# First stage with staging slots and a written order of its loads, the scan one projection later, and the roots of the first scales partly in PSUM

## The chip, the cores and the metric

The kernel runs on one core of a Trainium2 chip. The metric is the device time of one execution in microseconds (us). Three runs of the kernel before took 1379.6, 1372.67 and 1366.87 us, median 1372.67. The profiled execution is another one; it took 1369.38 us, and its span in the trace is 1367.0 us.

## The reference

One layer of a hybrid encoder on 2048 tokens of 1024 features, all in fp32. What bears on this case:

```python
hn   = rms_norm(h, norm_pre[i])            # h = x, 2048 x 1024
proj = hn @ w_in[i]                        # 1024 x 3072
u_s, z_s, q, k, v, z_n = jnp.split(proj, splits, axis=-1)    # 512 columns each
y_s  = s5_bidirectional(u_s, ...)          # 32 groups of 16 channels, a linear scan over the tokens each way
y_s  = gelu(y_s); y_s = y_s * sigmoid(y_s @ w_glu + b_glu) * silu(z_s)
y_n  = neighborhood_attention_2d(q, k, v, rpb) * silu(z_n)
h    = h + rms_norm(concat(y_s, y_n) @ w_out, norm_post)
h    = h + sigmoid(h @ w_gate) * rms_norm(p @ w_ple, ple_norm)
```

`rms_norm` divides each token's row by the root of its mean square; that root is a scale per token, which the kernel multiplies into the result of the projection.

## The kernel before, in words

**Matmuls in two parts.** Every fp32 matmul is made of three on rounded operands: x is split into a high part `xh` and a rest `xl`, and w into `wh` and `wl`. One result tile of 128 columns x 512 tokens takes 8 slices x 3 = 24 matmuls (`dense_steps`, L205). There are four blocks of 512 tokens, so one projection of 128 columns is 96 such matmuls.

**First stage** (`start`, L230). The first three projections (the u columns 0 to 383) run together, block by block: for each block b, 72 matmuls. `load_x` (L128) brings the transposed x of a block in 8 tiles (`xr`, L137) and splits each one: ACT rounds it (`xh`, L139), DVE takes the rest (`xl`, L140). `row_sums` (L145) brings the same tokens untransposed in 8 tiles (`xn`, L151), squares and sums them on ACT (L152), and DVE takes the inverse root by an integer guess and three Newton steps (`rsqrt_small`, L54: 13 instructions on 128 x 4 elements). `finish` then spreads the root over a PSUM bank with four small matmuls (`row_scale`, L163), ACT copies the bank to `rbc` (L166), and DVE multiplies the three result banks with it (`ev_u`, L267), which frees the banks. A block's results take three PSUM banks, and the block after next takes the same three (`pm` for even blocks; `pv` and two `qk` for odd ones). Each eviction is stored to DRAM through SP (`u_scr`, L270).

**Beside the first stage** POOL computes the tables of all scans (`ssm_tables`, L335), some 26 us for the first table `tab` (stored at L420) and 50 us more for `rot` (stored at L441).

**Then** `phase1` runs 18 projections: the fourth u tile, 4 of q, 4 of k, 4 of v, 4 of z_n, 1 of z_s. Before projection n, for n < 16, the code of scan n stands: `ssm_gen` (POOL builds the matrices `et`, `gt` and the rotations `ru` of two groups; PE turns `et` with L498 and makes a kernel with L505 and L507) and `ssm_scan` (PE brings in the states with L535, ACT copies them, and DVE runs the recurrence, L545 to L558). Its output matmuls (`ssm_out`, L567 to L569) are issued after the first block of the projection that follows. After phase 1 come the GLU, the attention and the output stages, which the change doesn't touch.

**What sets the order.** Each engine runs its instructions in a fixed order that a scheduler chooses when the kernel is built, from its own estimate of durations; `issue_after(i)` holds what stands under it behind instruction i in that order. An instruction that waits holds up all that stand behind it on its engine. All DMAs are issued by SP, in order as well.

Of the kernel before, what the change touches and what calls it, by code (L numbers as in the profile page):

```python
# [10 lines left out]
F32 = mybir.dt.float32  # L11
F32R = mybir.dt.float32r
I32 = mybir.dt.int32
AF = mybir.ActivationFunctionType
ALU = mybir.AluOpType
# [4 lines left out]
DM = 1024  # L20
# [13 lines left out]
NB = G // GB  # L34
GD = 2 * GB
EPS = 1e-6
# [14 lines left out]
class Layer:  # L51
# [70 lines left out]
    def last_pe(self):  # L122

        return next(i for i in reversed(self.nc.cur_bb.bb.instructions) if i.engine == mybir.EngineType.PE)


    def load_x(self, b):

        nc, a = self.nc, self.a
        th, tl = ("AA", "AA", "AB", "BC")[b]  # L130
        self.xh.append(self.slot(th, f"xh{b}", (128, KT, 512), F32R))
        self.xl.append(self.slot(tl, f"xl{b}", (128, KT, 512), F32R))
        xl, xh = self.xl[b], self.xh[b]
        xt = a["xT"].rearrange("(k p) t -> p k t", p=128)
        for k in range(KT):
            xr = self.xs.tile([128, 512], F32, tag="xr", name="xr", bufs=4)
            nc.sync.dma_start(xr, xt[:, k, 512 * b : 512 * b + 512])  # L137
            g = self.gpre[:, k : k + 1]
            nc.scalar.activation(xh[:, k, :], xr, AF.Copy, scale=g)  # L139
            nc.vector.scalar_tensor_tensor(xl[:, k, :], xr, g, xh.bitcast(F32)[:, k, :], ALU.mult, ALU.subtract)  # L140
            if k % 2:
                yield

    def row_sums(self, b):

        nc = self.nc
        ss = self.xs.tile([128, 4, 2], F32, tag="ss", name="ss", bufs=2)
        for i, e in itertools.product(range(4), range(2)):
            t = 512 * b + 128 * i
            xn = self.xs.tile([128, 512], F32, tag="xn", name="xn", bufs=3)  # L150
            nc.sync.dma_start(xn, self.a["x"][t : t + 128, 512 * e : 512 * e + 512])  # L151
            nc.scalar.activation(xn, xn, AF.Square, accum_out=ss[:, i, e : e + 1])  # L152
        var = self.xs.tile([128, 4], F32, tag="var", name="var", bufs=2)
        nc.vector.tensor_add(var, ss[:, :, 0], ss[:, :, 1])
        nc.vector.tensor_scalar(var, var, 1.0 / DM, EPS, ALU.mult, ALU.add)
        return self.rsqrt_small(self.xs, var, [128, 4], "rx")

    def row_scale(self, b, r):

# [70 lines left out]
    def start(self):  # L230

        nc, a = self.nc, self.a
        w = [self.w_tiles(self.xs if m == 2 else self.wp) for m in range(3)]
        x = self.load_x(0)
        for half in range(2):
            for m in range(3):
                self.load_half(w[m], 128 * m, half)
                if half == m == 0:
                    nc.sync.dma_start(self.gpre, a["gpre"])
                if m != 1:  # L240
                    next(x, None)
        nc.sync.dma_start(self.ident, a["ident"])
        self.ssm_tables()
        last = None

        def finish(b, r, ps):
            self.row_scale(b, r)
            for m in range(3):
                self.ev_u(m)(b, ps[m], self.rbc[:, 512 * b : 512 * b + 512])

        for b in range(4):
            if b < 3:
                self.run_steps(self.load_x(b + 1))
            r = self.row_sums(b)
            ps = []
            for m in range(3):
                ps.append(self.dense(w[m], b, tag=("pv", "qk", "qk")[m] if b % 2 else "pm"))
                if m == 1 and b:
                    finish(*last)
            last = b, r, ps  # L260
        finish(*last)
# [320 lines left out]
    def phase1(self):  # L582
        tc, nc = self.tc, self.nc
        self.es1 = es = ExitStack()
        P = lambda name, bufs, **kw: es.enter_context(tc.tile_pool(name=name, bufs=bufs, **kw))
        self.st = P("st", 1)
        self.rbc = self.st.tile([128, S], F32, name="rbc")
        self.wp = P("wp", 2)
        self.ev = P("ev", 3)
        with tc.tile_pool(name="xs", bufs=1) as self.xs, tc.tile_pool(name="gt", bufs=1) as self.gt:  # L590
            self.xh, self.xl = [], []
            self.start()
        jobs = [(384, self.ev_u(3))]
        for c, ev in ((1024, self.ev_q), (1536, self.ev_k), (2048, self.ev_v)):
            jobs += [(c + 128 * m, ev(m)) for m in range(4)]
        jobs += [(2560 + 128 * m, self.ev_z(self.zn_scr, m, 0.5)) for m in range(4)]
        jobs.append((512, self.ev_z(self.zs_scr, 0, 0.25)))
        with tc.tile_pool(name="sw", bufs=1) as self.sw:
            out = None
            for n in range(len(jobs)):  # L600
                scan = self.ssm_scan(n, *self.ssm_gen(n)) if n < NB else None
                self.project(*jobs[n], out)
                out = scan
        self.rt = self.ctx.enter_context(tc.tile_pool(name="rt", bufs=1, side="right"))
        tail = P("tail", 1)
        ws = [self.load_w(512 + 128 * m, tail if m == 3 else None) for m in range(1, 4)]
        self.tail = [(w, self.ev_z(self.zs_scr, m + 1, 0.25)) for m, w in enumerate(ws)]
        for b in range(2):
            for _ in self.zs(b):
                pass  # L610
# [474 lines left out]
```

## Time and profile before

| | before |
|---|---|
| runs | 1379.6, 1372.67, 1366.87 us, median 1372.67 |
| profiled execution, its span | 1369.38 us, 1367.0 us |
| mean granted clock of TensorE | 0.978 of full speed |
| busy share of the span | PE 95%, DVE 65%, POOL 41%, ACT 33% |
| PE idle, 180 to 372 us | 0.0 us |
| PE idle, 112.2 to 180 us | 11.6 us |
| DVE busy, 180 to 372 us | 171.75 of 192 us |
| POOL busy, 180 to 372 us | 148.70 of 192 us |

The page gives the busy time of each engine, the timeline gives every instruction with the idle time ahead of it and what ended that (the releaser), and the chain of waits follows the last instruction back to what released it. A matmul's busy time overlaps with that of the next; the pace is read from the starts.

### The profile page before, as it was taken

How to read it: one execution, taken by the hardware profiler on the slowest of the kernel's cores; microseconds unless marked ns; L12 is line 12 of the kernel's file. 1: busy time of each engine (PE TensorE's matmuls, PEld its weight loads, DVE VectorE, ACT ScalarE, POOL GpSimd, SP SyncE). 2: the span in 40 equal slices, each digit the busy share in tenths (PEclk: the TensorE clock that was granted, in tenths of full speed). 3: DMA queues.
4: the chain of work that ended last, by engine and by line, in shares of the span. 5: the costliest groups of instructions: out<-in, count | busy, mean ns of one | idle time of the engine just before them, and what ended most of it. 6: DMA issues, size and time to landing. Idle time of an engine off the chain costs nothing.

```text
span 1367.0 us, 19180 instructions
## 1 busy us (share of the span) xinstructions
PE 1299.8 (95%) x6496; PEld 1031.5 (75%) x6496; DVE 884.5 (65%) x1851; ACT 447.0 (33%) x957; POOL 554.1 (41%) x695
## 2 busy tenths in 40 slices
PE   7798999999999999999996898899999999999998
PEld 6676778888878888888664577777777888888886
DVE  5854899888977779623455565533333355888886
ACT  6631211111111122111565565544443223333322
POOL 5978888677766665000224344222220000211211
PEclk9998999999999999999998899999999999999999
DMA  8873223223333332216366575765526432343331
GB/s 278 251 220 84 79 81 100 82 84 106 88 79 88 75 85 77 91 67 192 117 216 239 175 241 178 236 212 175 180 93 214 164 108 70 105 131 116 102 126 62
DMA packets 183233, 186.86 MB, mean 137 GB/s; under 512 B 46944, under 2 KB 143584, under 8 KB 182496
## 3 DMA queue, kind: packets, MB, share of 16 engines
q1 hardware_dynamic: 183136, 185.65, 43.8%
q8 instruction: 51, 0.84, 0.3%
q14 instruction: 46, 0.38, 0.1%
HBM read 128.30 MB, written 57.31 MB: 136 GB/s over the span
## 4 chain that ended last, share of the span: by engine, by line
PE 76%; DVE 8%; DMA 7%; POOL 4%; issue 3%; ACT 2%; SPq 1%; DVEq 0%; ACTq 0%; POOLq 0%
PE pd L205 30%; PE pd L866 24%; PE p_qk L742 4%; PE p_qk L866 3%; PE p_pt L763 3%; PE po L779 3%; PE p_pt L535 2%; DMA raw<-in_w_out_dram 2%; PE pd L662 2%; DMA ys_scr<-zs 1%; PE p_pt L983 1%; DMA xn<-in_x_dram 1%; PE p_qk L568 1%; DMA wr<-in_w_in_dram 1%; DVE ev_u L267 1%
## 5 line engine op out<-in xcount | busy, mean ns | idle before, releaser
L205 PE MATMUL pd<-xh,wh 128*128 128x512 f32 x768 | 310.8, 406 | 15.1 <-DVE ev_u L267 7.7
L205 PE MATMUL pd<-xl,wh 128*128 128x512 f32 x768 | 308.0, 402 | 0.0
L205 PE MATMUL pd<-xh,wl 128*128 128x512 f32 x768 | 307.0, 400 | 0.0
L751 POOL TENSOR_SCALAR na<-na,rs 128x512 f32<-128x512 f32 (+1 forms) x128 | 88.3, 693 | 356.5 <-DVE rs L750 276.4
L205 PEld LDWEIGHTS pd<-xh,wh 128*128 128x128 f32 x768 | 145.5, 189 | 53.1 <-DVE ev_u L267 8.9
L205 PEld LDWEIGHTS pd<-xh,wl 128*128 128x128 f32 x768 | 145.4, 189 | 38.1 <-issue 4.0
L205 PEld LDWEIGHTS pd<-xl,wh 128*128 128x128 f32 x768 | 145.6, 190 | 35.3 <-issue 1.5
L1009 POOL TENSOR_TENSOR p3e<-p3e,p 128x1024 f32<-128x1024 f32 x15 | 39.1, 2608 | 292.1 <-DVE p3e L1004 285.4
L866 PE MATMUL pd<-wo,yh 128*128 128x512 f32 x512 | 143.7, 397 | 6.9 <-DVE o L901 3.5
L747 DVE CUSTOM_DVE_ANT_0 na<-p_qk,na 128x512 f32<-128x512 f32 (+1 forms) x128 | 75.2, 621 | 107.8 <-PE p_qk L742 105.5
L866 PE MATMUL pd<-wg,yh 128*128 128x512 f32 x512 | 140.7, 392 | 0.0
L866 PEld LDWEIGHTS pd<-wo,yh 128*128 128x128 f32 x512 | 96.7, 190 | 30.1 <-DVE o L901 4.8
L866 PEld LDWEIGHTS pd<-wg,yh 128*128 128x128 f32 x512 | 95.6, 188 | 19.1
L749 ACT ACTIVATE na<-na,mn 128x512 f32<-128x512 f32 (+1 forms) x128 | 84.8, 663 | 59.2 <-DVE mn L747 57.9
L764 ACT COPY na<-p_pt 128x512 f32<-128x512 f32 (+1 forms) x128 | 61.7, 529 | 71.7 <-PE p_pt L763 71.6
L866 PE MATMUL pd<-wo,yl 128*128 128x512 f32 x256 | 82.1, 396 | 0.0
L178 ACT ACTIVATE wh<-wr 128x512 fp32r<-128x512 f32 x48 | 28.2, 624 | 164.2 <-PE pd L205 158.5
L866 PE MATMUL pd<-wg,yl 128*128 128x512 f32 x256 | 81.4, 391 | 0.0
L763 PE MATMUL p_pt<-ident,na 128*128 128x128 f32 x448 | 64.3, 284 | 12.2 <-ACT na L764 6.4
L763 PEld LDWEIGHTS p_pt<-ident,na 128*128 128x128 f32 x448 | 51.9, 145 | 27.0 <-issue 16.4
L742 PE MATMUL p_qk<-na,na 64*128 64x512 f32 (+2 forms) x384 | 69.8, 461 | 0.8 <-DVE mn L747 0.8
L280 ACT ACTIVATE ev_th<-ev_z 128x512 f32<-128x512 f32 x32 | 20.1, 629 | 111.2 <-DVE ev_z L278 98.8
(205 smaller groups left out, 2311.5 us busy)
## 6 DMA issues: line engine op xcount, KB each, us to landing
wr<-in_w_in_dram SPq DMA_DIRECT2D x48, 256.0 KB
na<-in_bias_dram SPq DMA_DIRECT2D x8, 1152.0 KB
xr<-in_xT_dram SPq DMA_DIRECT2D x32, 256.0 KB
xn<-in_x_dram SPq DMA_DIRECT2D x32, 256.0 KB
o_scr<-o SPq DMA_DIRECT2D x16, 512.0 KB
p<-o_scr SPq DMA_DIRECT2D x16, 512.0 KB
xt<-in_x_dram SPq DMA_DIRECT2D x16, 512.0 KB
out_dram<-p3e SPq DMA_DIRECT2D x15, 512.0 KB
```

The source lines that it names most:

```text
L178: nc.scalar.mul(wh[:, sl], wr, mul)
L205: nc.tensor.matmul(ps, st[:, k, :], mv[:, k, :], start=n == 0, stop=n == 3 * KT - 1)
L535: nc.tensor.matmul(pv[:, NCH * g : NCH * g + NCH], win[:, GB * d + g, :], mv, start=True, stop=True)
L742: nc.tensor.matmul(ps[par][:, at : at + 32 * nr], q[own, 128 * j : 128 * j + 128], mv, start=True, stop=True)
L747: nc.vector.tensor_tensor_reduce(out=s, in0=ps[par][:, 0:n], in1=bm[:, par, (0, 1, 1, 2)[j], 0:n], scale=-1.0, scalar=3e38, op0=ALU.add, o ...
L749: nc.scalar.activation(s, s, AF.Exp, bias=mn, scale=-1.0, accum_out=sm)
L751: nc.gpsimd.tensor_scalar(s, s, rs, 1.0, ALU.mult, ALU.mult)
L763: nc.tensor.transpose(pt[:, x : x + 128], s[:, x : x + 128], self.ident)
L764: nc.scalar.copy(pT[:, n * j : n * j + n], pt[:, 0:n])
L779: self.nc.tensor.matmul(o, v[:, 4 * (rb if kt is None else kt) + jk, own], mv, start=first and rb == 0, stop=last and rb == wide - 1, skip ...
L866: nc.tensor.matmul(ps[e], st[:, k, :], mv[k][:, 512 * e : 512 * e + 512], start=k == 0 and n == 0, stop=k == nk - 1 and n == 2)
L1009: nc.gpsimd.tensor_add(th, th, h1)
```

## The change

Three edits.

- **Staging and order in the first stage.** The transposed tiles of blocks 0, 1 and 2 land in 16 staging slots (`stageB`, `stageC`, slots of the pools B and C that hold other data later); those of block 3 and all `xn` tiles share a ring of 7 (before: 4 for `xr` and 3 for `xn`). The loads' order is now written: x of blocks 0 and 1, then sums of block 0, x of block 2, sums of 1, x of 3, sums of 2, sums of 3, each behind the SP instruction that stood last.
- **Roots.** `row_sums` computes the same root with `var`, `t` and `i` in a PSUM bank and only `r` in SBUF, in 14 instructions where there were 13. `rsqrt_small` stays for the later stages.
- **Scan one projection later.** Scan n-1 now stands before projection n, for n = 1 to 16, and its output matmuls in projection n+1.

```diff
--- before.py
+++ after.py
@@ -123,6 +123,10 @@
 
         return next(i for i in reversed(self.nc.cur_bb.bb.instructions) if i.engine == mybir.EngineType.PE)
 
+    def last_of(self, engine):
+
+        return next(i for i in reversed(self.nc.cur_bb.bb.instructions) if i.engine == engine)
+
 
     def load_x(self, b):
 
@@ -133,7 +137,7 @@
         xl, xh = self.xl[b], self.xh[b]
         xt = a["xT"].rearrange("(k p) t -> p k t", p=128)
         for k in range(KT):
-            xr = self.xs.tile([128, 512], F32, tag="xr", name="xr", bufs=4)
+            xr = next(self.stage) if b < 3 else self.xs.tile([128, 512], F32, tag="xr", name="xr", bufs=7)
             nc.sync.dma_start(xr, xt[:, k, 512 * b : 512 * b + 512])
             g = self.gpre[:, k : k + 1]
             nc.scalar.activation(xh[:, k, :], xr, AF.Copy, scale=g)
@@ -147,13 +151,24 @@
         ss = self.xs.tile([128, 4, 2], F32, tag="ss", name="ss", bufs=2)
         for i, e in itertools.product(range(4), range(2)):
             t = 512 * b + 128 * i
-            xn = self.xs.tile([128, 512], F32, tag="xn", name="xn", bufs=3)
+            xn = self.xs.tile([128, 512], F32, tag="xr", name="xn", bufs=7)
             nc.sync.dma_start(xn, self.a["x"][t : t + 128, 512 * e : 512 * e + 512])
             nc.scalar.activation(xn, xn, AF.Square, accum_out=ss[:, i, e : e + 1])
-        var = self.xs.tile([128, 4], F32, tag="var", name="var", bufs=2)
-        nc.vector.tensor_add(var, ss[:, :, 0], ss[:, :, 1])
-        nc.vector.tensor_scalar(var, var, 1.0 / DM, EPS, ALU.mult, ALU.add)
-        return self.rsqrt_small(self.xs, var, [128, 4], "rx")
+        V = nc.vector
+
+        bank = self.ps2("pt")
+        var, t, i = (bank[:, 4 * n : 4 * n + 4] for n in range(3))
+        r = self.xs.tile([128, 4], F32, tag="rx", name="rx", bufs=2)
+        V.tensor_reduce(var, ss, mybir.AxisListType.X, ALU.add)
+        V.tensor_scalar(var, var, 1.0 / DM, EPS, ALU.mult, ALU.add)
+        V.tensor_scalar(i.bitcast(I32), var.bitcast(I32), 1, None, ALU.arith_shift_right)
+        V.tensor_scalar(r.bitcast(I32), i.bitcast(I32), -1, 0x5F3759DF, ALU.mult, ALU.add)
+        V.tensor_scalar(var, var, -0.5, None, ALU.mult)
+        for _ in range(3):
+            V.tensor_mul(t, var, r)
+            V.tensor_mul(t, t, r)
+            V.scalar_tensor_tensor(r, t, 1.5, r, ALU.add, ALU.mult)
+        return r
 
     def row_scale(self, b, r):
 
@@ -230,6 +245,8 @@
     def start(self):
 
         nc, a = self.nc, self.a
+        stage = [self.slot(t, "stage" + t) for t in "BC"]
+        self.stage = itertools.cycle([s[:, 512 * i : 512 * i + 512] for s in stage for i in range(8)])
         w = [self.w_tiles(self.xs if m == 2 else self.wp) for m in range(3)]
         x = self.load_x(0)
         for half in range(2):
@@ -248,10 +265,13 @@
             for m in range(3):
                 self.ev_u(m)(b, ps[m], self.rbc[:, 512 * b : 512 * b + 512])
 
+        self.run_steps(self.load_x(1))
         for b in range(4):
-            if b < 3:
-                self.run_steps(self.load_x(b + 1))
-            r = self.row_sums(b)
+            with self.tc.issue_after(self.last_of(mybir.EngineType.SP)):
+                r = self.row_sums(b)
+            if b < 2:
+                with self.tc.issue_after(self.last_of(mybir.EngineType.SP)):
+                    self.run_steps(self.load_x(b + 2))
             ps = []
             for m in range(3):
                 ps.append(self.dense(w[m], b, tag=("pv", "qk", "qk")[m] if b % 2 else "pm"))
@@ -598,7 +618,7 @@
         with tc.tile_pool(name="sw", bufs=1) as self.sw:
             out = None
             for n in range(len(jobs)):
-                scan = self.ssm_scan(n, *self.ssm_gen(n)) if n < NB else None
+                scan = self.ssm_scan(n - 1, *self.ssm_gen(n - 1)) if 0 < n <= NB else None
                 self.project(*jobs[n], out)
                 out = scan
         self.rt = self.ctx.enter_context(tc.tile_pool(name="rt", bufs=1, side="right"))
```

How it moves the instructions, at three places. First ACT, around its first `rbc` copy (L166 before, L181 now), which the evictions of block 0 need. Buffers `xh_658` and `xh_710` are the high parts of blocks 2 and 3. Before:

```order
L152 ACTIVATE xn,ss<-xn 128x512
L139 ACTIVATE xh_658<-xr,gpre 128x512
L152 ACTIVATE xn,ss<-xn 128x512
L139 ACTIVATE xh_658<-xr,gpre 128x512 x2
L152 ACTIVATE xn,ss<-xn 128x512
L166 COPY rbc<-p_pt 128x512
L152 ACTIVATE xn,ss<-xn 128x512
L139 ACTIVATE xh_824<-xr,gpre 128x512
L152 ACTIVATE xn,ss<-xn 128x512
L139 ACTIVATE xh_824<-xr,gpre 128x512 x2
```

Now:

```order
L156 ACTIVATE xn,ss<-xn 128x512 x8
L143 ACTIVATE xh_568<-stageB,gpre 128x512 x8
L156 ACTIVATE xn,ss<-xn 128x512 x8
L143 ACTIVATE xh_710<-xr,gpre 128x512 x2
L181 COPY rbc<-p_pt 128x512
L143 ACTIVATE xh_710<-xr,gpre 128x512 x6
L156 ACTIVATE xn,ss<-xn 128x512 x8
L181 COPY rbc<-p_pt 128x512
```

Before, the copy stood behind all of block 2's `xh` and five of the eight squares of block 1's sums, in turns. Now it stands behind all eight squares of block 1's sums and the first two tiles of block 3.

Second SP, around the store of the first table (`tab_scr`, L420 before, L440 now), which waits for POOL. Before:

```order
L151 DMA xn<-in_x_dram 128x512
L137 DMA xr<-in_xT_dram 128x512
L420 DMA tab_scr<-tab 128x1280
L137 DMA xr<-in_xT_dram 128x512
L151 DMA xn<-in_x_dram 128x512 x2
L137 DMA xr<-in_xT_dram 128x512
L151 DMA xn<-in_x_dram 128x512
L137 DMA xr<-in_xT_dram 128x512 x2
L151 DMA xn<-in_x_dram 128x512
```

Now:

```order
L141 DMA stageB<-in_xT_dram 128x512 x8
L155 DMA xn<-in_x_dram 128x512 x7
L440 DMA tab_scr<-tab 128x1280
L155 DMA xn<-in_x_dram 128x512
L141 DMA xr<-in_xT_dram 128x512 x8
L290 DMA u_scr_71<-ev_u 1024x1x64
L290 DMA u_scr_72<-ev_u 1024x1x64
L290 DMA u_scr_73<-ev_u 1024x1x64
```

Tiles for the sums and transposed tiles took turns behind the store; now one `xn` tile of block 1 (its eighth) and all of block 3 stand behind it, and the loads of blocks 2 and 3 for the sums stand behind the stores of the evictions.

Third PE, where the first generator's matrices are turned (L498 before, L518 now). Before, after 384 matmuls of the projections:

```order
L205 MATMUL pd<-xl_825,wh 128x512
L205 MATMUL pd<-xh_824,wl 128x512
L498 MATMUL p_qk<-ident,et 128x128 x4
L535 MATMUL p_pt<-u,win 128x256 x4
L505 MATMUL p_qk<-gt,y_1148 16x128
L507 MATMUL p_qk<-gt,y_1148 16x128
L505 MATMUL p_qk<-gt,y_1148 16x128
L507 MATMUL p_qk<-gt,y_1148 16x128
L205 MATMUL pd<-xh_168,wh 128x512
L205 MATMUL pd<-xl_169,wh 128x512
L205 MATMUL pd<-xh_168,wl 128x512
```

Now, after 390 of them:

```order
L220 MATMUL pd<-xh_170,wh 128x512
L220 MATMUL pd<-xl_171,wh 128x512
L220 MATMUL pd<-xh_170,wl 128x512
L518 MATMUL p_qk<-ident,et 128x128 x2
L220 MATMUL pd<-xh_170,wh 128x512
L220 MATMUL pd<-xl_171,wh 128x512
L220 MATMUL pd<-xh_170,wl 128x512
L220 MATMUL pd<-xh_170,wh 128x512
L220 MATMUL pd<-xl_171,wh 128x512
L518 MATMUL p_qk<-ident,et 128x128 x2
L220 MATMUL pd<-xh_170,wl 128x512
```

The turns, and the state matmuls L535 (L555 now), stood between the fourth projection and the fifth's first block as one block of work; now they stand inside the fifth projection, L555 after 409. The first output matmuls (L567 before, L587 now) stand after 454 and after 504 projection matmuls. The small scale matmuls (L163 before, L178 now) stood after 134, 192, 264 and 312 projection matmuls; now they stand after 144, 216 and 288, the last two blocks' together.

## Rows read from the trace of the kernel before

**Rows 1.** Page, busy time of each engine and its share of the span (first part).
```profile
PE 1299.8 (95%) x6496; PEld 1031.5 (75%) x6496; DVE 884.5 (65%) x1851; ACT 447.0 (33%) x957; POOL 554.1 (41%) x695
```

**Rows 2.** Waits of PE from 0 to 200: who, for whom: us, times, longest.
```profile
PE pd L205 <- DVE ev_u L267: 7.7, 2, 5.3
PE pd L205 <- ACT xh L139: 7.5, 1, 7.5
PE p_qk L498 <- POOL et L479: 4.8, 3, 1.8
```

**Rows 3.** Chain, steady projections: start us, us, what, count.
```profile
202.93 16.80 PE pd L205 x72
...
228.65 0.43 PE p_qk L567 x2
...
231.24 16.80 PE pd L205 x72
```

**Rows 4.** Timeline of PE at the end of the fourth projection.
```profile
112.20 0.39 PE L205 MATMUL pd<-xh,wl 128*128 128x512 f32 x1
```

**Rows 5.** Timeline of PE: start us, us, what, [idle before, releaser].
```profile
42.39 1.16 PE L163 MATMUL p_pt<-ident,rxr 128*128 128x128 f32 x8 [1.67 <-DVE rxr L67]
43.30 0.48 PE L205 MATMUL pd<-xh,wl 128*128 128x512 f32 x1
...
51.21 0.79 PE L205 MATMUL pd<-xh,wh 128*128 128x512 f32 x1 [5.33 <-DVE ev_u L267]
...
55.21 0.43 PE L205 MATMUL pd<-xh,wh 128*128 128x512 f32 x1
```

**Rows 6.** Windows: busy us of engines (instructions), granted clock, DMA share, GB/s.
```profile
50.00:60.00 10.00, 8.79 (x30) 7.01 (x31) 9.68 (x14) 5.85 (x15) 9.92 (x20) 0.74 1.00 272
112.20:180.00 67.80, 56.18 (x230) 42.96 (x229) 56.25 (x85) 11.71 (x19) 57.95 (x66) 0.90 0.29 78
```

**Rows 7.** Timeline of POOL: end of the tables, first generator.
```profile
90.84 1.60 POOL L440 TENSOR_SCALAR rot<-rot,sgn 128x1600 f32<-128x1600 f32 x1
...
104.31 1.07 POOL L490 TENSOR_TENSOR ru<-rt 128x512 f32<-128x512 f32 x1 [5.47 <-DMA rt<-rot_scr]
...
115.50 0.72 POOL L479 TENSOR_TENSOR et<-et,gtmp 128x256 f32<-128x256 f32 x1
...
126.20 0.32 POOL L462 TENSOR_TENSOR y<-y,y 128x64 f32<-128x64 f32 x1
```

**Rows 8.** Chain of waits, 40 to 52: start us, us, what, count.
```profile
41.09 1.24 POOL tab L419
...
42.35 0.33 SPq L420
...
43.25 5.51 DMA xn<-in_x_dram
...
49.57 0.48 ACT rbc L166
```

**Rows 9.** Timeline of ACT: copies of a tile and squares.
```profile
47.95 0.72 ACT L139 ACTIVATE xh<-xr,gpre 128x512 fp32r<-128x512 f32 x1 [3.74 <-DMA xr<-in_xT_dram]
...
51.18 0.61 ACT L152 ACTIVATE xn<-xn 128x512 f32<-128x512 f32 x1
```

**Rows 10.** Timeline of DVE: evictions and steps of the roots.
```profile
50.07 3.12 DVE L267 TENSOR_TENSOR ev_u<-pd,rbc 128x512 f32<-128x512 f32 x3 [0.62 <-ACT rbc L166]
...
58.71 0.61 DVE L65 TENSOR_TENSOR rxt<-rxr 128x4 f32<-128x4 f32 x1
...
91.00 1.47 DVE L62 TENSOR_SCALAR rxi<-var 128x4 int32<-128x4 int32 x1
...
92.78 0.16 DVE L65 TENSOR_TENSOR rxt<-rxr 128x4 f32<-128x4 f32 x1
```

**Rows 11.** Timeline of DVE: first and last step of the first scan.
```profile
121.95 0.74 DVE L545 STREAM_SHUFFLE sw<-x 128x512 f32<-128x512 f32 x1
...
144.14 0.74 DVE L558 TENSOR_TENSOR x<-x,t 128x508 f32<-128x508 f32 x1
```

## Prediction

> **What bounds the kernel now.** I read the page's busy shares first: PE is busy for 95% of the span [rows 1], so a change can only win where PE stands still or runs slowly. The waits of PE for the first 200 us say where: 7.5 us until the first tile, 7.7 us for evictions (the longest 5.3), 4.8 us for the generators' matrices [rows 2]. Then the chain in the steady part: 72 projection matmuls take 16.80 us, 0.2333 us each, and one projection with one scan comes every 231.24 - 202.93 = 28.31 us [rows 3]. Of these, 96 x 0.2333 = 22.40 are the projection, so a scan costs PE 5.91 us, and of them its output matmuls 231.24 - 228.65 = 2.59 [rows 3]. No wait stands between those rows: from 202.93 on phase 1 is PE's own work, and the change takes none of it away. What can be won lies ahead of 202.93.
>
> How much is lost there, in two stretches. **A**, from PE's first matmul (7.45, after the first wait [rows 2]) to the 384th projection matmul at 112.20 [rows 4]. Its work is 384 x 0.2333 = 89.6 us and four sets of scale matmuls at 43.30 - 42.39 = 0.91 [rows 5], 93.2 in all; it took 104.8, so 11.5 us are lost. [...] **B**, from 112.20 to 202.93. In it stand 216 projection matmuls (50.4 us), three whole scans (17.7) and one without its outputs (3.3), 71.4 us of work in 90.7: 19.3 us are lost, in waits and in a mean clock of 0.90 [rows 6].
>
> **The scan one projection later.** B is lost because PE meets the first generator at the 384th matmul, at 112.20, while POOL has its matrices only at 115.50 + 0.72 = 116.2 [rows 7], and because each step behind it (states, copy, scan, outputs) then comes too late for the next. Now PE has 390 matmuls ahead of the first turn and 504 ahead of the first outputs (454 before). I take the whole 19.3 back if each step is in time, and check that after A, whose end it needs.
>
> **Staging and the written order.** I follow what releases PE at its 144th matmul, the first one of block 2, which needs block 0's banks free. The chain before: POOL ends the first table at 42.33, SP stores it at 42.35, behind the store a load is issued at 43.25 and lands 5.51 us later, ACT squares it, copies the scale (ends at 50.05), DVE evicts, PE goes on at 51.21 [rows 5, 8]. The load just ahead of it was there at 47.95, when ACT took it [rows 9]. The change leaves this chain: POOL's order is the same up to there, SP still has loads behind the store that the first copy waits for, and these are now three: the last square of block 1 and two tiles of block 3. With the landings of before, the first at 47.95 and the next two at the pace of those rows (48.76 - 47.95, 0.8 us), ACT takes the last tile at 49.6 (0.72), copies from 50.4 to 50.9, and DVE, with two root steps and a tile ahead, evicts from some 51.8; the first of three evictions takes 3.12 / 3 = 1.04 [rows 10]. PE goes on at about 53.0, 1.8 us **later** than before. The 16 staging slots let the loads run ahead, but PE cannot use it: it is at its 144th matmul by 42 to 46 in either kernel (7.45 + 33.6 + 0.91 = 42.0 at the earliest, 5.33 ahead of 51.21 before) and stands there. Bounds: released as before (51.2), or one landing of 5.51 later (58.5). I take 53.0, since the rows are of the same transfers. The clock behind this stall I take as before, 1.9.
>
> The next two boundaries are new. The scale matmuls of block 1 stood 48 matmuls (11 us) ahead of the banks' next use; now they stand right ahead of it. So PE waits for copy and eviction: 0.6 + 1.04 + 0.2 of hand-over, 1.8 us, at 53.0 + 1.9 + 72 x 0.2333 + 0.91 = 72.6. It goes on at 74.4 and is through block 3 at 91.2. There it makes the scales of blocks 2 and 3 (1.8, to 93.0), and block 3's needs its root: its loads stand on SP behind the stores of block 1's evictions (to 76.3), its eight squares on ACT (0.61 each [rows 9]) behind weights that become free at 80.0 and 85.6, so the sums are there at some 87.3. Fourteen root steps follow, and a weight tile of about 0.9. A step on 128 x 4 took 0.16 with POOL still and 0.61 beside it [rows 10]; on PSUM none is shown. At 0.25 the root is there at 91.8, PE has not waited, and the copy and eviction of block 2 let it go on at 94.0, 0.9 lost; at 0.61 it is 97 and 4 us more. I take 0.25, nearer to 0.16, as no step has a second SBUF operand now.
>
> On the roots the rows show the contention itself: a one-operand step took 1.47 us at 91.00, and ended just as POOL's 1.60 us instruction from 90.84 did [rows 7, 10]. [...]
>
> So the 384th matmul comes at 94.0 + 96 x 0.2333 = 116.4, **4.2 us later** than at 112.20.
>
> **Is B free then?** POOL's first matrices are there at 116.2 at the latest, PE asks for them at 117.8. DVE starts the first scan behind a step that needs POOL's second `y`, at 126.5 [rows 7]; the scan took 121.95 to 144.88, 22.9 us [rows 11], so it ends at 149.4. PE asks for it after 120 matmuls (28.0) and two scans' entries (6.6), at 151.0. In time, by 1.6 us. Later scans have 28.31 us each for some 23 to 24 on DVE. If these covers go, it costs up to 3 us. At the other end nothing is added: the last outputs go to projection 17, well ahead of the GLU that reads them.
>
> **Sum**: -19.3 + 4.2 = -15.1 us against the profiled execution of 1369.38: 1354.3. The median shown is 3.3 higher, so the same gain from there gives 1357.6. I forecast 1356, between the two.
>
> **Rivals.**
> 1. *The boundaries eat it* (same). If each of the two new boundaries costs what the first did, 5.33 + 1.9 in place of 1.8 and 0.9, that is 11.8 more: gain 3.3, about 1367. For it: ACT and SP are in order, and each block's loads now wait for the last one's evictions. Against it: I find the copies free to start when the scale matmuls end. A first scan 3 us late lands between this and the forecast.
> 2. *The first stall shrinks* (faster). If POOL ends its first table earlier, everything up to 53.0 moves with it. Of what A wins so, B's cover lets only 1.6 count, until DVE's first scan binds; that scan hangs on POOL as well, and comes earlier by as much as POOL does. With POOL 4 us earlier the gain is 15.1 + 1.6 + 4 = 20.7, about 1349. For it: nine two-operand steps of each root no longer stand against POOL, at 0.16 to 0.61 each 1.4 to 5.5 us a root. Against it: the splits of the tiles stay, three times as much DVE work with two SBUF operands. [...]
> 3. *Loads one by one* (slower). The last two blocks' sums now stand behind the stores of evictions, in a ring of seven. If the last block's eight loads land one after another at 5.51 us [rows 8], from 76.8, the sums come at 121, PE goes on at 128 in place of 94.0: 34 more, 19 slower, 1388. It decides from 3.5 us a load on, where the gain is gone. Against it: 0.8 us from one landing to the next in the rows used above.
> 4. *Nothing done*: were the first scan held by DVE and not by PE's order, B would stay and A's 4.2 be added, 1374. Against it: what PE waits for there is POOL, 4.8 us [rows 2].
>
> **Chances.** Forecast 0.52, boundaries 0.22, smaller stall 0.18, one by one 0.03, nothing done 0.05. About 1% (13.7 us) is what a measurement of this kernel can tell from no change; below 1359 counts as faster. The forecast's own range is 1350 to 1362 (landing, root and cover), two thirds of it below 1359. So faster 0.35 + 0.18 = 0.53; same 0.17 + 0.22 + half of "nothing done" = 0.42; slower 0.05. Eight in ten: 1346 to 1369, the smaller stall at one end, the boundaries at the other.
>
> **What would show it.** PE's wait for the first `ev_u` should end near 53, with short ones of 1 to 2 us near 72.6 and 93; the 384th matmul near 116; no wait for POOL's `et`, and none over 1 us for a scan's `x`; 28.3 us per projection from then on. The forecast is wrong if `rbc` does not wait on loads behind the table's store, or if waits for `et` or `x` stand beyond 118.

## The result and the profile after

The changed kernel takes 1354.4 us in the median of four runs (1351.04 to 1359.12); the kernel before, in four runs, 1371.01. The ratio is 0.9878 with a 95% interval of 0.9832 to 0.9923: faster, by 10.6 to 23 us, 16.6 in the medians. Ratios, here and below, leave out a run that stood over 1.5% above the fastest of its kernel (in the experiments 1372.87 of the later scan alone, and 1390.39 and 1391.68 of the kernel before), while medians keep it. The profiled executions lie closer together: spans of 1357.3 and 1367.0 us, 9.7 apart; the changed kernel's, at 1359.12 us, was the slowest of its four runs.

PE's waits, for whom, us in total, times and longest, from 0 to 210, answer to [rows 2]:

```profile
PE p_pt L178 <- DVE rx L170: 7.9, 2, 6.5
PE pd L220 <- ACT xh L143: 7.5, 1, 7.5
PE pd L220 <- DVE ev_u L287: 6.1, 2, 4.2
```

All waits for POOL's `et` and `gt` and for the scan's `x` are gone; a wait for a root, 6.5 us long, is new. The timeline of PE shows where (start, duration, [idle before, releaser]); it answers to [rows 4, 5] and to the first row of [rows 3]:

```profile
45.32 1.16 PE L178 MATMUL p_pt<-ident,rx 128*128 128x128 f32 x8 [1.36 <-DVE rx L170]
50.69 0.79 PE L220 MATMUL pd<-xh,wh 128*128 128x512 f32 x1 [4.21 <-DVE ev_u L287]
...
71.93 0.47 PE L220 MATMUL pd<-xh,wh 128*128 128x512 f32 x1 [1.87 <-DVE ev_u L287]
...
88.78 1.05 PE L178 MATMUL p_pt<-ident,rx 128*128 128x128 f32 x8
96.36 2.07 PE L178 MATMUL p_pt<-ident,rx 128*128 128x128 f32 x8 [6.52 <-DVE rx L170]
98.08 0.77 PE L220 MATMUL pd<-xh,wh 128*128 128x512 f32 x1
...
121.93 0.39 PE L220 MATMUL pd<-xh,wl 128*128 128x512 f32 x1
...
123.56 0.38 PE L518 MATMUL p_qk<-ident,et 128*128 128x128 f32 x2
...
156.83 0.59 PE L587 MATMUL p_qk<-u,m 128*128 128x256 f32 x2
...
187.55 0.58 PE L220 MATMUL pd<-xh,wh 128*128 128x512 f32 x1
```

The turn at 123.56 stands after 390 projection matmuls; the row at 121.93 is the 384th. The row at 187.55 follows the second outputs and answers to 202.93 before, with 600 projection matmuls done in either; one scan less has been entered by then, so 5.91 us are added: 193.5. Up to here 9.5 us are won, nearly all of the spans' 9.7. By stage: A is 9.7 us longer than before (121.93 against 112.20), B 19.2 shorter (187.55 - 121.93 + 5.91 = 71.5, against 202.93 - 112.20 = 90.73). From there on six projections take 28.32 us each, as in the kernel before.

The windows (length, busy us of PE, PEld, DVE, ACT and POOL, then the granted clock, the DMA share and GB/s) answer to the second part of [rows 6]: in B the clock is now at 1.00, where it was 0.90 up to 180.

```profile
50.00:60.00 10.00, 9.31 (x34) 7.44 (x35) 9.02 (x17) 4.93 (x11) 9.92 (x20) 0.81 0.93 254
98.08:120.50 22.42, 22.42 (x91) 17.97 (x91) 8.44 (x10) 0.59 (x1) 13.98 (x23) 0.92 0.75 190
120.50:190.00 69.50, 69.50 (x318) 55.95 (x317) 58.48 (x88) 12.62 (x21) 54.63 (x62) 1.00 0.30 87
```

In B the first matrices and the first scan's end, on POOL and DVE, answer to [rows 7, 11]:

```profile
116.16 0.73 POOL L499 TENSOR_TENSOR et<-et,gtmp 128x256 f32<-128x256 f32 x1
...
153.14 0.69 DVE L578 TENSOR_TENSOR x<-x,t 128x508 f32<-128x508 f32 x1
```

They end 6.7 and 3.0 us before PE asks (123.56, 156.83). What set the first restart, on POOL, SP and ACT, answers to [rows 8, 9]:

```profile
40.26 0.75 POOL L439 TENSOR_SCALAR tab<-tab,sgn 128x576 f32<-128x576 f32 x1
...
41.03 0.33 SPq L440 DMA_DIRECT2D tab_scr<-tab  x1
41.45 0.38 SPq L155 DMA_DIRECT2D xn<-in_x_dram  x1
...
46.49 0.63 ACT L156 ACTIVATE xn<-xn 128x512 f32<-128x512 f32 x1 [3.48 <-DMA xn<-in_x_dram]
...
48.54 0.56 ACT L181 COPY rbc<-p_pt 128x512 f32<-128x512 f32 x1
```

It is the chain that the prediction followed, table, store, load, square, copy, only 1.3 us earlier on POOL and with a load that was there 5 us after its issue. The third boundary's rows, on DVE and SP, answer to the second half of [rows 10]:

```profile
78.22 10.72 DVE L194 SCALAR_TENSOR_TENSOR wl<-wr,wh 128x512 fp32r<-128x512 f32 x2 [4.26 <-ACT wh L193]
91.86 0.69 DVE L194 SCALAR_TENSOR_TENSOR wl<-wr,wh 128x512 fp32r<-128x512 f32 x1 [2.92 <-ACT wh L193]
92.66 0.17 DVE L162 TENSOR_REDUCE p_pt<-ss 128x4 f32<-128x8 f32 x1
...
96.14 0.16 DVE L170 SCALAR_TENSOR_TENSOR rx<-p_pt,rx 128x4 f32<-128x4 f32 x1
...
88.24 0.39 SPq L192 DMA_DIRECT2D wr<-in_w_in_dram  x1
88.72 0.46 SPq L155 DMA_DIRECT2D xn<-in_x_dram  x1
```

The fourteen root steps took 0.16 to 0.17 us each, here with POOL still, and in the root of block 1 beside POOL as well (DVE, POOL):

```profile
47.24 0.17 DVE L162 TENSOR_REDUCE p_pt<-ss 128x4 f32<-128x8 f32 x1 [1.98 <-ACT xn L156]
...
46.59 1.31 POOL L433 TENSOR_TENSOR cm<-rot 128x64 f32<-128x64 f32 x4
```

But ahead of them two weight splits, 0.69 each with POOL idle, stood for 10.72 while POOL made the table, 9.99 of it the first of the two; SP's next weight load waited for the buffer of that one until 88.24, and behind that load stood the last `xn` of block 3. So the sums were there at 92.5 only. From 84.0 to 88.2, while the split stood, no DMA ran and ACT did nothing; POOL and PE were busy throughout:

```profile
84.00:88.20 4.20, 4.20 (x20) 3.37 (x19) 4.20 (x2) 0.00 (x0) 4.20 (x10) 1.00 0.00 0
```

### The profile page after: what moved, and what is told of

Read it like the earlier page. It is cut to its first block, busy times and chain, and to the rows that moved or that the text cites. A ratio compares the mean times of both kernels' runs of the same rounds, so it can differ in the third digit from the quotient of the medians.

```text
span 1357.3 us, 19152 instructions
## 1 busy us (share of the span) xinstructions
PE 1295.8 (95%) x6496; PEld 1029.2 (76%) x6496; DVE 889.6 (66%) x1855; ACT 445.2 (33%) x957; POOL 552.2 (41%) x695
## 5 line engine op out<-in xcount | busy, mean ns | idle before, releaser
L575 DVE TENSOR_TENSOR_SCAN t<-rt,t 128x128 f32<-128x128 f32 x64 | 61.1, 1014 | 0.6
```

The source lines that it names most:

```text
L575: V.tensor_tensor_scan(v[:, i], rt[:, 0, i, NROT - 1 : NROT].to_broadcast([128, NPR]), v[:, i], 0.0, ALU.mult, ALU.add)
```

## Experiments

Four kernels were timed together each time, against the kernel before, whose medians in the three sets were 1369.98, 1367.98 and 1367.82 (23, 11 and 17 runs). The edits are against the changed kernel unless said otherwise.

### The edits apart

**The later scan alone** (the kernel before, plus:)

```diff
-                scan = self.ssm_scan(n, *self.ssm_gen(n)) if n < NB else None
+                scan = self.ssm_scan(n - 1, *self.ssm_gen(n - 1)) if 0 < n <= NB else None
```

> The kernel before with the third edit alone: the scan one projection later, the first stage as it was. If the gain comes from PE's order behind the 384th projection matmul, that matmul stays at 112.2 us; PE asks for the first turned matrices six matmuls later, at 113.7, and waits some 2.5 us for POOL (116.2), and nothing else is lost until the steady part: 14 to 17 us gained, about 1355, the changed kernel's time or a little less. Rival: the later scan needs the later first stage of the change as its cover (POOL and the first scan are then not late); then waits for the generators and for the scan's results stand between 112 and 200 us, and the gain is under 8 us, 1363 or more.

Measured: 1353.94 (6 runs), ratio 0.9872 (0.9824 to 0.9919), the changed kernel's own. PE's only wait behind the 384th matmul is for the first scan's end:

```profile
152.95 0.70 PE L568 MATMUL p_qk<-x,gt 128*128 128x256 f32 x2 [1.96 <-DVE x L558]
```

The expected wait of 2.5 us for POOL did not come: the 384th matmul stood at 113.87, the scheduler put the first turn behind 411 projection matmuls and not 390, at 120.40, and POOL's matrices were there at 117.77. So B was a matter of PE's order, and the later scan needs nothing of the rest.

**Staging, order and roots without the later scan** (that diff undone):

> The changed kernel with the scan back at its old place: staging, written order and roots alone. In the changed kernel's profile the 384th matmul came at 120.9 us where it was at 112.2 before. If these edits are a loss that the later scan pays for, the time is 1371 to 1380: the 8.7 us are lost, less what PE then waits less for POOL's first matrices, up to 4.8 and the scan behind them. [...]

Measured: 1365.02 (12 runs), ratio 0.9953 (0.9927 to 0.9978): not the loss that I had expected. (The changed kernel's 384th matmul came at 121.93, not 120.9.) PE waits for `et` (2.8), the scans (4.4) and `win` (1.0) stand in B again. That it is nevertheless some 6 us faster than before by the ratio (5 in the medians) is not in its profile: the attention's first `po` matmul, which stands behind the whole of phase 1, comes at 673.69, and at 670.70 and 675.77 in two profiles of the old first stage. Its twelve runs lie within 4 us, those of the kernel before, without the one left out, over 17; it may cut the late ones, which was not shown. Beside the later scan the first two edits add nothing that can be told: 0.9878 with them, 0.9872 without.

**The old roots** (13 steps, all in SBUF, in the changed kernel):

```diff
-        bank = self.ps2("pt")
-        var, t, i = (bank[:, 4 * n : 4 * n + 4] for n in range(3))
...
+        nc.vector.tensor_add(var, ss[:, :, 0], ss[:, :, 1])
+        nc.vector.tensor_scalar(var, var, 1.0 / DM, EPS, ALU.mult, ALU.add)
+        return self.rsqrt_small(self.xs, var, [128, 4], "rx")
```

> The changed kernel with the roots of the first stage in the old form, thirteen steps all in SBUF, nine of them with two SBUF operands. If only the long splits (128x512, two SBUF inputs) suffer beside POOL, and the roots are bound by what stands ahead of them, the time stays within 3 us of the changed kernel's 1354. Rival: each of the nine steps stands beside POOL as the split of 10.7 us for two did (78 to 89 us of the changed kernel's profile); then each boundary of the first stage comes several us later, 1360 to 1370.

Measured: 1375.55 (12 runs), ratio 1.0024 (0.999 to 1.0058): 21 us more than the changed kernel; my theory falls, by more than its rival said. DVE, and PE behind it:

```profile
55.23 15.95 DVE L158 TENSOR_TENSOR var<-ss 128x4 f32<-128x4 f32 x1
80.05 6.11 DVE L66 SCALAR_TENSOR_TENSOR rxt<-rxt,var 128x4 f32<-128x4 f32 x1
...
88.24 2.08 PE L167 MATMUL p_pt<-ident,rxr 128*128 128x128 f32 x8 [21.68 <-DVE rxr L67]
```

An addition of 128 x 4 elements with two SBUF operands stood 16 us beside POOL, another step 6.11, and the written order has put PE right behind them.

**The new roots and the later scan in the old order** (the kernel before with these two edits):

> The kernel before with two of the three edits: the later scan and the roots with at most one SBUF operand; loads and buffers as before, no written order. With the later scan alone (1353.9) PE still waited 5.6 us for an eviction near 52, 2.4 for roots and 2.0 for the first scan's end. If the roots matter in this order too, the waits for roots go (2.4 us) and the time is 1350 to 1353. Rival: with the old order the roots are not what anyone waits for, 1353 to 1355; then the 21 us that the old roots cost in the written order are a matter of that order alone.

Measured: 1354.12 (6 runs), ratio 0.9881 (0.9831 to 0.9932): by the time, the rival. Its profile had a long split again:

```profile
62.04 14.58 DVE L140 SCALAR_TENSOR_TENSOR xl<-xr,gpre,xh 128x512 fp32r<-128x512 f32 x2
```

PE had waited 15.1 us for an eviction by then (until 60.08), which is not that split's doing: the copy ahead of the eviction ran at 58.25 only, as the scheduler had chosen another order of loads and squares here. So no worth of the roots shows outside the written order, but the order did not stay the old one either, and what they are worth in that is not shown.

### The boundaries

**The table's store later on SP** (`nc.sync.dma_start(self.tab_scr, tab)` moved to behind `load_x(3)`):

> The changed kernel with the store of the first table moved on SP from ahead of block 1's last tile for the sums to behind the transposed loads of block 3. In the changed kernel PE waited 4.21 us until 50.69 for the first eviction, behind a copy that stood behind loads issued after that store (41.45). If the store sets that stall, PE goes on at 47 to 49, as soon as the first root (45.3), the copy and one eviction allow. The third boundary hangs on other work (a split that stands beside POOL until 89, a load behind it), so I expect it to end at 97 to 99 as before and the time within 2 us of 1354. Rival: everything behind the first stall moves with it: third boundary at 95, time 1350 to 1352.

Measured: 1351.3 (6 runs), ratio 0.9869 (0.9818 to 0.9919). In the profile both things came: the first restart at 48.95, the third boundary where it was (PE went on at 98.18).

```profile
48.95 0.79 PE L220 MATMUL pd<-xh,wh 128*128 128x512 f32 x1 [2.72 <-DVE ev_u L290]
...
96.48 2.04 PE L178 MATMUL p_pt<-ident,rx 128*128 128x128 f32 x8 [7.46 <-DVE rx L170]
```

The store does set the first stall, and the third boundary takes back what that gives. The 3 us in the median are within the interval.

**The weight loads behind the last tile on SP**:

```diff
+        if col == 384:
+            w = self.load_w(col)
+        else:
+            with self.tc.issue_after(self.last_xn):
+                w = self.load_w(col, mul=0.125 if 1024 <= col < 1536 else 1.0)
```

> The changed kernel with the weight loads from the sixth projection tile on held on SP behind the last tile for block 3's sums. In the changed kernel's profile that tile was issued at 88.72, behind a weight load that waited for the buffer of a split standing beside POOL until 88.94; the third boundary ended at 98.08. If that order on SP is the cause, the last square comes at some 84, the reduce right behind the split at 89 and PE goes on at 93 to 95. The time gains less than the 4 us, since the first scan's end (153.8, set by POOL's matrices) then is what PE waits for: 1351 to 1353. Rival: the boundary stays at 97 to 99 because the split itself, not the load, holds DVE; then 1354.

Measured: 1353.89 (6 runs), ratio 0.9871 (0.9821 to 0.9922); the boundary stayed (PE went on at 98.32). The theory that SP's order alone is the cause falls:

```profile
80.05 10.14 DVE L194 SCALAR_TENSOR_TENSOR wl<-wr,wh 128x512 fp32r<-128x512 f32 x2 [4.30 <-ACT wh L193]
90.11 0.16 DVE L162 TENSOR_REDUCE p_pt<-ss 128x4 f32<-128x8 f32 x1
93.43 0.69 DVE L194 SCALAR_TENSOR_TENSOR wl<-wr,wh 128x512 fp32r<-128x512 f32 x1 [2.56 <-ACT wh L193]
...
96.59 2.08 PE L178 MATMUL p_pt<-ident,rx 128*128 128x128 f32 x8 [4.93 <-DVE rx L170]
```

The reduce did come right behind the split, but DVE's order has the next weights' split between the root's steps, and that now waited for its load.

**The two splits on POOL**:

```diff
+        if col == 384:
+            nc.gpsimd.tensor_sub(wl[:, sl], wr, wh.bitcast(F32)[:, sl])
```

> The changed kernel with the two weight splits that stood on DVE from 78.22 to 88.94 made by POOL, in its own order between the table's steps. If these splits, starved beside POOL, set the third boundary, DVE reduces block 3's sums some 8 us earlier and PE goes on at 91 to 94 in place of 98.08. POOL is 3 to 4 us later with its tables, so its first matrices come at 119 to 121 where PE now asks at 115 to 118: what the boundary gives is taken again, 1352 to 1357. Rival: the boundary stays at 98 (something other than the splits and POOL holds it): 1354 to 1358, with POOL's delay on top.

Measured: 1355.6 (6 runs), ratio 0.9893 (0.9842 to 0.9945). POOL needs 1.3 us for a split, block 3's root starts at 86.87 (92.66 in the changed kernel), and the boundary is what the prediction had made of it:

```profile
80.37 1.30 POOL L195 TENSOR_TENSOR wl<-wr,wh 128x512 fp32r<-128x512 f32 x1
82.31 1.31 POOL L195 TENSOR_TENSOR wl<-wr,wh 128x512 fp32r<-128x512 f32 x1
...
92.37 1.16 PE L178 MATMUL p_pt<-ident,rx 128*128 128x128 f32 x8 [0.65 <-DVE rx L170]
93.51 0.50 PE L223 MATMUL pd<-xh,wh 128*128 128x512 f32 x1
```

PE is there at 90.67 and goes on at 93.5 (forecast: 94.0); beyond the scale matmuls 1.0 us is lost, for a forecast 0.9. So the splits on DVE were the cause of the long boundary. POOL's first matrices came at 117.5, not 119 to 121. PE now waits 1.2 us for the first scan's end (until 154.06); the attention's first `po` matmul comes at 656.9, against 661.57 in the changed kernel. The time does not show it, within the scatter that comes next.

### The scatter

**A measurement behind the last output**: four splits on DVE alone, four beside POOL's multiplications, four with one input in PSUM beside them; in a second kernel POOL's steps are smaller and don't wait for each other.

```diff
+        dve(at(2), at(0), at(1))
+        pool(at(2, 128))
+        dve(at(2), at(0), at(1))
+        V.tensor_copy(at(3), at(5))
+        pool(at(3, 128))
+        dve(at(2), at(3), bank)
```

> The changed kernel with a measurement appended behind its last output: four splits of 128x512 on DVE with two SBUF inputs and nothing beside them; four more beside 25 POOL multiplications of 128x128; four with one input in PSUM beside 25 such multiplications. If POOL's back-to-back work starves a DVE instruction with two SBUF inputs, the first four take 0.7 us each, the second four together as long as POOL's chain (some 10 us) or most of it, the third four 0.7 to 0.8 each. Rival: the 10.7 us in the first stage came from something else (DMA traffic, ACT's writes): then all twelve take 0.7 to 1. The appended part lengthens the kernel by some 30 us, which says nothing. The same run shows a second time whether the split between 78 and 89 us stands as long, and the third boundary's end (98.08).

> The measurement behind the last output again, with POOL multiplications of 128x64 on independent outputs, 24 in a row, so that they follow each other as closely as the table's steps did (0.28 us from start to start). Before, with 0.53 us from start to start, DVE's four splits took 3.27 us beside POOL and 2.86 alone: POOL gave way. If a DVE instruction with two SBUF inputs gets in only where POOL leaves a gap between two instructions, the second group of four now takes 5 to 8 us, most of POOL's chain, and the third, with one input in PSUM, still 2.9. Rival: POOL gives way again (3.0 to 3.5 us); then what starved the splits in the first stage is not POOL's closeness alone, and stays open. The same profile repeats the changed kernel's first stage a third time.

Measured: 1387.32 and 1378.7 us with the appended parts. The rival both times, POOL gives way (DVE and POOL of the second kernel):

```profile
1353.28 2.86 DVE L1045 SCALAR_TENSOR_TENSOR port<-port 128x512 f32<-128x512 f32 x4
1356.77 2.87 DVE L1045 SCALAR_TENSOR_TENSOR port<-port 128x512 f32<-128x512 f32 x4 [0.63 <-POOL port L1048]
1365.92 2.85 DVE L1045 SCALAR_TENSOR_TENSOR port<-port,p_pt 128x512 f32<-128x512 f32 x4
...
1356.82 8.53 POOL L1050 TENSOR_TENSOR port<-port 128x64 f32<-128x64 f32 x24
1366.43 6.69 POOL L1050 TENSOR_TENSOR port<-port 128x64 f32<-128x64 f32 x24
```

Beside splits with two SBUF inputs POOL's 24 steps took 8.53 us, beside those with one in PSUM 6.69: the two do contend. But nothing stood for 10 us. The measurement does not repeat the first stage in one thing: DVE's first split began 0.05 us ahead of POOL's chain (1356.77, 1356.82), where in the first stage POOL's chain was already running. The rival's other causes, DMA traffic and ACT's writes, do not fit: the split of the changed kernel stood from 84.0 to 88.2 with neither of them at work. Nor does PE, which was busy: with PE busy and POOL idle two splits took 1.29 us (at 92.64, in the changed kernel with the hold, below). What lets POOL keep a split out there stays open.

The two profiles repeat the changed kernel's first stage: the two splits took 7.74 and 10.47 us, and PE went on from the third boundary at 98.46 and 98.58 (98.08).

**POOL's products held in the GLU**, in the kernel before, the changed one, and the one with the later scan alone. The scheduler had changed the order of a few instructions in the attention too, and in the kernel before PE waited 5.2 us for one of them there.

```diff
-                nc.gpsimd.tensor_mul(v[e], v[e], ge)
+                with self.tc.issue_after(self.last_of(mybir.EngineType.Pool)):
+                    nc.gpsimd.tensor_mul(v[e], v[e], ge)
```

> The kernel before, with one edit far behind the change: in the GLU, POOL's products `zs` are held behind the POOL instructions written ahead of them (scales `na` of the attention's scores). In the profiled executions so far the change is 9.1 us ahead when the first `po` matmul of the attention starts (661.6 against 670.7 us), while the medians differ by 16.6; in the kernel before, one `na` stands on POOL behind a `zs` that waits for a load until 776, and PE waits 5.2 us for it (780.60), and in the changed kernel the scheduler put it ahead. Theory: that order is worth the rest of the medians' difference, so this kernel takes 1362 to 1365 where the kernel before takes 1368 to 1371. Rival: the attention's length only scatters from run to run (356.7 and 364.4 us in two profiles of the changed order); then 1368 to 1371.

> The changed kernel with the same hold on POOL. With the same order of POOL in the attention as the run beside it, the two differ by the first stage alone: 9 us by the profiles, so 1352 to 1356. By the rival, that the medians' 16.6 us all come from the first 660 us, 1346 to 1354 with the other run at 1362 to 1370, still 16 apart.

> The kernel before with the later scan alone, and the hold on POOL. The later scan alone reached the first `po` matmul at 655.8 us, 5.8 earlier than the changed kernel, at an equal median (1353.9 and 1354.4), with POOL's attention order of the kernel before. If that order cost it the difference, 1345 to 1349, faster than both kernels. Rival (scatter): 1352 to 1356.

Measured: before 1366.3 (12 runs), ratio 0.9982 (0.9951 to 1.0012); changed 1355.32 (6 runs), 0.9887 (0.9842 to 0.9932); later scan alone 1349.88 (6 runs), 0.9858 (0.9802 to 0.9914). The first lies between theory and rival, the third as well, and the order there is worth nothing that can be told: the theory is not borne out. The two kernels with equal orders behind the first stage are 11 us apart, nearer to the profiles' 9.7 than to 16.6. These profiles repeat the first stages, instruction for instruction in the same order up to 300 us:

| first stage of | first `po` matmul, us | attention, first to last `po`, us |
|---|---|---|
| before (before, with the hold) | 670.70, 675.77 | 365.8, 360.9 |
| changed (changed, two with the measurement, with the hold) | 661.57, 661.67, 662.29, 667.93 | 364.6, 356.9, 360.4, 362.0 |
| later scan alone (without, with the hold) | 655.81, 655.45 | 362.5, 359.5 |

The same order of instructions comes up to 6.4 us apart (661.57 and 667.93). The rows that make it so, of the changed kernel with the hold, DVE and PE:

```profile
52.97 19.91 DVE L144 SCALAR_TENSOR_TENSOR xl<-xr,gpre,xh 128x512 fp32r<-128x512 f32 x3
...
76.39 2.08 PE L178 MATMUL p_pt<-ident,rx 128*128 128x128 f32 x8 [6.74 <-DVE rx L170]
84.38 0.77 PE L220 MATMUL pd<-xh,wh 128*128 128x512 f32 x1 [5.91 <-DVE ev_u L287]
```

The first of the three splits took 18.36 us of this; in the changed kernel it took 0.89. Of the kernel before with the hold the row is this; its two splits took 0.97 and 0.93 in the profile that the prediction read:

```profile
84.17 6.75 DVE L184 SCALAR_TENSOR_TENSOR wl<-wr,wh 128x512 fp32r<-128x512 f32 x2 [4.08 <-ACT wh L183]
```

Which split stands beside POOL, and for how long, differs from execution to execution. The attention adds a scatter of its own (356.9 and 364.6 with one order).

The best median is that of the later scan alone with the hold, 1349.88. Its interval overlaps with the changed kernel's, so it is not shown to be faster; by the profiles its first stage is 6 us ahead of the changed kernel's.

## Why the prediction was right, and where it was not

The time (1354.4 for 1356), the direction, and the mechanism of the gain were right; the sum was not made of the terms that I had.

- **B: the gain was right, its cover was not.** Forecast 71.4 us of work with nothing lost, measured 71.5. POOL's `et` was there at 116.16 + 0.73, PE asked at 123.56. The first scan ended at 153.8, 4.4 us later than my 149.4 (it started at 132.2 for 126.5). It was in time only because A was late and PE asked at 156.83 and not at 151.0; with the splits on POOL, where the 384th matmul came at 115.78, PE waited 1.2 us for it. The experiment with the later scan alone shows that this edit by itself gives the gain.
- **A: mis-sized, 9.7 us later than before where I had 4.2** (4.0 by exact count: 94.0 + 96 x 0.2333 is the 385th matmul). The first stall was the chain that I followed and ended 2.3 us sooner, as POOL's table came 1.3 earlier and the load landed sooner; the second boundary's wait was 1.87 for 1.8, and PE went on at 71.93 for 74.4. The 1.9 us that the sum has for the clock behind the first stall is nine matmuls in 4.00 us [rows 5] for 9 x 0.2333, at a granted clock of 0.50 from 51.2 to 55.2; in the changed kernel seven matmuls took 3.15 us from 50.69, for 1.63, so 1.5 was lost (granted clock 0.50 up to 52.80).
- **The step that failed is the third boundary**, 0.9 us in the prediction. PE was there at 88.78, had 1.8 of scale matmuls, and went on at 98.08: 7.5 lost, and 1.7 more behind it at a low clock (102 matmuls took 25.5 us up to 123.56 for 23.8; granted clock 0.92 up to 120.50). I had block 3's sums at 87.3 and took "a weight tile of about 0.9" for the split ahead of the root; the split stood until 88.94, and the sums, whose last load stood behind it on SP, were there at 92.5. The root's steps were not it (0.16 to 0.17 each for my 0.25). The boundary ended between 98.1 and 98.6 in three of the four profiles of this order, and with the two splits on POOL at 93.5, on the forecast.
- **The price of the roots.** The 0.16 to 0.61 us for a step in SBUF from [rows 10] belong to the old order of the loads: in its four profiles no step took over 1.5 us. In the one profile of the written order one such step took 15.95, and without the edit on the roots that order gave no gain at all, the later scan included (ratio 1.0024). The 0.25 that the sum took for a step without a second SBUF operand was an estimate of mine between the two of [rows 10], and no run shows it; on PSUM, where no row had shown a price, a step took 0.16 to 0.17 in the changed kernel, with POOL still (from 92.66) and beside it (from 47.24).
- **Rival 2** came in part: POOL ended its first table 1.3 us earlier, not 4. Its point against itself, that the tiles' splits stay, was the right worry in the wrong place: it concerned POOL, and DVE paid. That two-operand steps on DVE hold POOL up was an assumption there; the runs show it for splits (8.53 us for POOL's 24 steps, for 6.69 beside splits with one input in PSUM), for the roots' steps it was not shown.
- **Rival 1** was half true: A came 9.7 us later where it needed 16, and not by SP's and ACT's order alone, but through DVE's splits. Rivals 3 and 4 did not occur.
- **That the sum came out near is not explained by its terms.** In the profiled pair the gain is 9.7 where the sum said 15.1, short by A's 5.5. The medians say 16.6, those of the two kernels with the hold 11.0, and the interval is 10.6 to 23. Whether the forecast met the time by its terms or by scatter is open. I had treated the first stage of one profile as a constant.

## What to carry to other kernels

Where PE waits because it meets a producer too early, moving the consumer later in PE's order can be the whole gain, as here (ratio 0.9872 with that edit alone), and it is read as work against elapsed time in that stretch. Buffers and a written order that put PE directly behind small steps on another engine make that engine's worst instruction count, so price such a step by the longest row of its kind beside the busy neighbour, not by the typical one (here 15.95 us for an addition of 128 x 4, where no step of the old order had taken over 1.5). Before a gain of 1% is taken apart, profile the same order twice: the first `po` matmul moved by up to 6 us here.

## What the runs showed of the hardware that I had not expected

- A DVE instruction with two SBUF operands can stand 6 to 18 us beside POOL's table steps. Two weight splits (0.69 us each with POOL idle) took 7.7 to 11.5 us in all six profiles of the written order in which DVE made them beside these steps, nearly all of it one of the two; elsewhere one `xl` split took 18.36, one 13.85, and an addition of 128 x 4 15.95. Other executions of the same order had 0.89 for the `xl` split of 18.36, and 0.97 for a weight split of 6.15. The wait is longer than one POOL instruction: 23 of POOL's began in the 9.99 us of the changed kernel's split (from 78.22).
- Instructions with at most one SBUF operand and the rest in PSUM did not: 0.15 to 0.18 us for every step of the new roots in all nine profiles that have them, beside POOL or not.
- A measurement of the pairing by itself, with DVE first, did not show the long wait: 2.87 us for four splits beside POOL, 2.86 alone, and POOL gave way (8.53 for 6.69 us).
